# Split weights of seven tiles kept between two column parts of a decoder layer

## The chip, the cores and the metric

The kernel runs on one core of a Trainium2 chip. The metric is the device time of one execution in microseconds (us); a version is timed by the median of several runs.

Five engines with queues of their own work beside each other and meet at semaphores: TensorE (PE: matmuls, with its weight loads shown as PEld), VectorE (DVE), ScalarE (ACT), GpSimd (POOL) and SyncE (SP, which here issues nearly all loads from memory). Each queue is run in its written order: an instruction that waits holds up what stands behind it.

## The reference

One layer of a decoder: two branches (a gated linear recurrence and a chunked gated linear attention) are merged by learned gates into `m`; then come an output projection, a norm and a SwiGLU feed-forward net. The part that matters here is this:

```python
m = jax.nn.sigmoid(u_ga) * (y_a @ proj_a) + jax.nn.sigmoid(u_gb) * (y_b @ proj_b)
x = (x + gt1 * (m @ w_out)).astype(x.dtype)
h2 = _rmsnorm(x, norm2_g) * (1.0 + sc2) + sh2
f1, f2 = jnp.split(h2 @ ffn_w1, 2, axis=-1)
x = (x + gt2 * ((jax.nn.silu(f1) * f2) @ ffn_w2)).astype(x.dtype)
```

The model width is 1024, the hidden width of the feed-forward net is 2816. There are 1024 prompt tokens and 8 sequences of 4 sample tokens; everything is float32.

## The kernel before

Activations are kept transposed: features in the 128 partitions, tokens in the columns. The tokens go through the whole layer in two halves, A (512 prompt tokens) and B (512 prompt tokens and the 32 sample tokens). A tile name ends in the letter of its half: `woa` is the output projection's weight tile in half A, `wob` in half B.

A matrix product in float32 is made of three faster ones. An operand is split into a rounded high part and the rest: ACT copies it into the format `F32R` (the high part), and DVE subtracts that from the original (the low part). Three matmuls, high by high, high by low and low by high, make the product; in `gemm` they are lines 407, 408 and 409, and the third is the one that reads the low part of the weights. So a weight tile of 128x1024 costs one load of 512 KB into a buffer of the tag `raw` (5 buffers), one copy on ACT (line 150, with line 151 in `split_w`) and one subtraction on DVE (line 151) into a buffer of the tag `hl` (3 buffers). The `raw` buffer comes free when the subtraction is done, the `hl` buffer when the last matmul that uses it is done.

After the branches each half runs `merge_a` and then `back`. `merge_a` makes the eight tiles of `m`, one at a time, from a gate product (`gaps`, weights `gaps_hl`), and a product of 5 + 5 blocks (`paps`, weights `pa0`, `pa1`) with the ten tiles `ya`; the last, j = 7, ends with two operations on DVE (lines 1165 and 1166, on `ga7`) and the split of `m7` (ACT line 184, DVE line 185). `back` works on two column parts of the half, each 256 columns in A and 272 in B:

- `out_proj` on the first part (tiles `wo` of weights j = 0 to 7 in rising order), then on the second (j = 7 to 0). Each result gets the residual (`xr`, loaded for it by SP) added on DVE (line 1193 or 1182) and is squared on ACT for the norm.
- `norm2` of the first part, woven into the second part of `out_proj`, makes the eight tiles `h2` (DVE line 473, ACT line 486, DVE line 487).
- `ffn1_first` does the first four pairs of feed-forward tiles ("narrow couples", f = 0 to 3; weights `f1`, `f2`, results in `f1ps`, `f2ps`), first on part one, in rising order, with `norm2` of part two woven in; then on part two in falling order.

So each weight tile of `out_proj` and of the narrow couples is needed twice. `load_kept` lets the last three tiles before the turn stay in their `hl` buffers; all others are loaded and split a second time. That makes five tiles of `wo` (j = 4 to 0) and five of the couples (`f1` of f = 2, 1, 0 and `f2` of f = 1, 0) in each half.

Large tiles (two times 544 columns) come from a pool with the tag `S` and 17 buffers; `ya`, `yb`, `m`, the results `fa` of the couples and the blocks `t12`, `t4` of the next stage are all in it. A new tile takes the buffer that came free first, and its writer waits for the last reader of the tile that was there.

What is written is the program order; a scheduling layer then places the instructions in each engine's queue by their priority and by when it believes them ready. `tc.high_priority(AHEAD)` moves a piece 70 places forward in priority.

Of the kernel before, what the change touches and what calls it, by code (L numbers as in the profile page):

```python
# [7 lines left out]
F32 = mybir.dt.float32  # L8
F32R = mybir.dt.float32r
I32 = mybir.dt.int32  # L10
AF = mybir.ActivationFunctionType
# [6 lines left out]
KD = 8  # L18
# [11 lines left out]
EARLY = 4  # L30
FAST = 6
KORD = (0, 2, 4, 6, 1, 3, 5, 7)
AHEAD = 70
# [21 lines left out]
def hybrid_layer(ctx, tc, I, O):  # L55
    nc = tc.nc
    pe, act, dve, pool, sp = nc.tensor, nc.scalar, nc.vector, nc.gpsimd, nc.sync
# [21 lines left out]
    def S(name, dt=F32):  # L79
        return sbig.tile([P, 2 * 544], dt, tag="S", name=name)  # L80

    def T(name, w=544):
        return tp.tile([P, w], F32, tag="t", name=name)
# [12 lines left out]
    def mm(name):  # L96
        return mmk[1].tile([P, mmk[0], 512], F32, tag="mm", name=name)
# [41 lines left out]
    def load_raw(src, n, name):  # L139
        raw = wp.tile([P, 1024], F32, tag="raw", name=name + "_raw", bufs=5)  # L140
        sp.dma_start(raw[:, :n], src)
        return raw

    def load_w(src, n, name):
        return split_w(load_raw(src, n, name), n, name)

    def split_w(raw, n, name):
        hl = wp.tile([P, 2, 1024], F32R, tag="hl", name=name + "_hl", bufs=3)
        with tc.high_priority(AHEAD):
            act.activation(hl[:, 0, :n], raw[:, :n], AF.Copy)  # L150
            dve.tensor_sub(hl[:, 1, :n], raw[:, :n], hl[:, 0, :n].bitcast(F32))  # L151
        return hl

    held = {}

    def load_kept(key, src, n, name, last):

        if key in held:
            return held.pop(key)
        hl = load_w(src, n, name)  # L160
        if last:
            held[key] = hl
        return hl

    def split_apart(raw, n, name):

        hi, lo = S(name + "_hi", F32R), S(name + "_lo", F32R)
        act.activation(hi[:, :n], raw, AF.Copy)
        dve.tensor_sub(lo[:, :n], raw, hi[:, :n].bitcast(F32))
        return Apart(hi, lo)  # L170

    class Apart:
# [185 lines left out]
    class Half:  # L358
# [159 lines left out]
        def begin(s):  # L518
# [26 lines left out]
            def weights(i):  # L545
                hl[i] = (split_w if i < 3 else split_apart)(raws[i], 1024, f"early{ts[i]}")
# [650 lines left out]
        def out_proj(s, part, acc):  # L1197
            o, w = part[0], part[1]
            for q in range(KD):
                j = q if o == 0 else KD - 1 - q  # L1200
                n = f"{s.n}{o}{j}"
                xt = T("xr" + n)
                sp.dma_start(xt[:, :w], I["x" + s.n][:, j * s.N + o:j * s.N + o + w])
                ps = mm("wops" + n)
                s.gemm(ps, load_kept(("wo", j), I["w_out"][j], 1024, "wo" + n, o == 0 and j >= KD - 3), 8, s.m, part=part)
                if o == 0:
                    s.x.append(xp.tile([P, 544], F32, tag="X", name="xm" + n))
                with tc.high_priority(AHEAD):
                    s.residual(s.x[j], ps, 2, j, xt, part, "w" + n)
                    s.add_sq(acc, s.x[j][:, o:o + w], w, q, "2" + n)  # L1210
                yield w * 24 / 2400.0
# [9 lines left out]
        def pair(s, f, part, a):  # L1221

            n = f"{s.n}{f}{part[2]}{part[0]}"
            whole = part[2] is None
            gp = None if whole else part
            o, w = part[0], part[1]
            p1 = s.wide("f1ps" + n) if whole else mm("f1ps" + n)
            fr = not whole and o == 0
            s.gemm(p1, load_kept(("f1", f), I["ffn1"][2 * f], 1024, "f1" + n, fr and f == EARLY - 1), 8, s.h2, part=gp, order=KORD)
            yield w * 24 / 2400.0  # L1230
            tg = T("ft" + n)[:, :w]
            ps = [(tg[:, p[0] - o:p[0] - o + p[1]], p) for p in s.pieces(part)]
            for t, p in ps:
                act.activation(t, s.psv(p1, p), AF.Tanh, scale=0.5)
                dve.scalar_tensor_tensor(t, t, 1.0, s.psv(p1, p), op0=OP.add, op1=OP.mult)
            p2 = s.wide("f2ps" + n) if whole else mm("f2ps" + n)
            s.gemm(p2, load_kept(("f2", f), I["ffn1"][2 * f + 1], 1024, "f2" + n, fr and f >= EARLY - 2), 8, s.h2, part=gp, order=KORD)
            for t, p in ps:
                dve.tensor_mul(t, t, s.psv(p2, p))
            hi, lo = a[:, o:o + w], a[:, s.N + o:s.N + o + w]  # L1240
            act.activation(hi, tg, AF.Copy)
            dve.tensor_sub(lo, tg, hi.bitcast(F32))
            yield w * 24 / 2400.0

        def block_sums(s):
# [4 lines left out]
            for i in range(4):  # L1250
                h0, h1 = s.h2[2 * i], s.h2[2 * i + 1]
                d0, d1, ta, tb = [T(f"{c}{s.n}{i}") for c in ("d0", "d1", "ta", "tb")]
                for d, h in (d0, h0), (d1, h1):
                    dve.tensor_add(d[:, :N], h[:, :N].bitcast(F32), h[:, N:2 * N].bitcast(F32))
                dve.tensor_sub(ta[:, :W], d0[:, :W], d0[:, W:N])
                dve.tensor_sub(ta[:, W:N], d1[:, :W], ta[:, :W])
                dve.tensor_sub(tb[:, :W], d1[:, :W], d0[:, :W])
                dve.tensor_sub(tb[:, W:N], d1[:, W:N], ta[:, W:N])
                pair = lambda t: (t[:, :N], t[:, N:2 * N])
                if i == 0:  # L1260
                    t3 = pair(tp.tile([P, 2 * 544], F32R, tag="m2t", name="t3" + s.n, bufs=1))
                if i == 2:
                    t3 = [tp.tile([P, 544], F32R, tag="acc", name=f"t3{c}{s.n}", bufs=2) for c in "hl"]
                if i % 2 == 0:
                    t4 = pair(S(f"t4{s.n}{i}", F32R))
                t12 = pair(S(f"t12{s.n}{i}", F32R))
                o4 = i % 2 * W
                for t, o, src in (t12, 0, ta[:, :N]), (t4, o4, tb[:, W:N]), (t3, o4, tb[:, :W]):
                    w = N if t is t12 else W
                    act.activation(t[0][:, o:o + w], src, AF.Copy)  # L1270
                    dve.tensor_sub(t[1][:, o:o + w], src, t[0][:, o:o + w].bitcast(F32))
                for k, t, o in (("11", pair(h0), W), ("21", pair(h1), W), ("22", pair(h1), 0), ("t1", t12, 0), ("t2", t12, W),
                                ("t3", t3, o4), ("t4", t4, o4)):
                    s.bs[k].append((t[0][:, o:o + W], t[1][:, o:o + W]))
                yield 10
# [210 lines left out]
    p0, p1 = B.halves  # L1486
# [111 lines left out]
```

## Time and profile before

| | |
|---|---|
| median of 3 runs | 1983.96 us (1980.19 to 1984.69) |
| time of the profiled execution | 1982.02 us |
| its span, from first to last instruction | 1980.3 us |
| granted TensorE clock, mean | 0.994 |
| PE busy | 1948.1 us, 98% of the span |
| PEld busy | 1775.3 us, 90% |
| DVE busy | 1252.2 us, 63% |
| ACT busy | 914.9 us, 46% |
| read from memory | 259.16 MB |

PE is busy in all but 32 us of the span. A share over the whole span says little of one stage; the stage from `merge_a`'s end to the end of `ffn1_first` lies at about 551 to 664 us in half A and 1532 to 1650 us in half B. The matmul ends in the trace are modelled, so the distance between two starts is the better measure of PE's pace.

### The profile page before, as it was taken

Reading aid. Unit: us, or ns where it says so; the run is one execution under the profiler, and the core shown is the slowest. Engines: PE = TensorE matmul, PEld = TensorE weight load, DVE = VectorE, ACT = ScalarE, POOL = GpSimd, SP = SyncE. Lnnn points to the kernel's source line nnn. Section 1 sums busy time; section 2 is a strip of 40 time slices with the busy share of each in tenths; the row PEclk is TensorE's granted clock in tenths of the full one; section 3 lists DMA queues with packets and bytes.
Section 4 is the critical chain, followed back from the end, with each engine's and each line's share of the span. In section 5 each row is a group of like instructions: output and inputs, shape, how many; then the busy total and the mean of one; then the engine's idle time right before and its main releaser. Section 6 shows DMA issues by size and latency. Waiting matters only on the chain. (4 is left out here: it accounts for less than half of the span.)

```text
span 1980.3 us, 33359 instructions
## 1 busy us (share of the span) xinstructions
PE 1948.1 (98%) x13524; PEld 1775.3 (90%) x13524; DVE 1252.2 (63%) x2126; ACT 914.9 (46%) x1377; POOL 74.4 (4%) x159
## 2 busy tenths in 40 slices
PE   9999999999999999999999999999999999999998
PEld 5877877776899998998899999899999999999997
DVE  5648487656458764778563697774343687636776
ACT  3646475533235542555352465563232354415553
POOL 0000011000000000000000001010000000000000
PEclk9999999999999999999999999999999999999999
DMA  8334235566644457554413223323233434435553
GB/s 338 98 105 165 70 107 201 189 245 246 219 161 139 148 186 246 183 171 145 160 65 99 104 70 101 108 83 105 70 91 106 159 126 139 138 104 170 173 156 117
DMA packets 106906, 287.34 MB, mean 145 GB/s; under 512 B 12288, under 2 KB 20224, under 8 KB 106752
## 3 DMA queue, kind: packets, MB, share of 16 engines
q1 hardware_dynamic: 98608, 257.20, 39.9%
q0 software_dynamic: 7600, 27.45, 3.7%
q8 instruction: 106, 1.74, 0.4%
q10 hardware_dynamic: 544, 0.56, 0.1%
q14 instruction: 48, 0.39, 0.1%
HBM read 259.16 MB, written 26.01 MB: 144 GB/s over the span
## 5 line engine op out<-in xcount | busy, mean ns | idle before, releaser
L151 DVE TENSOR_TENSOR fwa_hl<-fwa,fwa_hl 128x1024 fp32r<-128x1024 f32 (+1 forms) x57 | 68.8, 1207 | 44.6 <-ACT fwa_hl L150 41.2
L151 DVE TENSOR_TENSOR fwb_hl<-fwb,fwb_hl 128x1024 fp32r<-128x1024 f32 (+1 forms) x57 | 68.7, 1206 | 39.9 <-ACT fwb_hl L150 35.5
L150 ACT ACTIVATE fwa_hl<-fwa 128x1024 fp32r<-128x1024 f32 (+1 forms) x57 | 59.2, 1039 | 44.0 <-PE fapsa L1305 10.8
L150 ACT ACTIVATE fwb_hl<-fwb 128x1024 fp32r<-128x1024 f32 (+1 forms) x57 | 59.3, 1040 | 33.3 <-PE fcpsb L1305 8.0
L150 ACT ACTIVATE f3b_hl<-f3b_raw 128x768 fp32r<-128x768 f32 (+1 forms) x45 | 35.7, 794 | 74.5 <-PE f3psb L409 21.4
L407 PE MATMUL f3psa<-faa,f3a_hl 128*128 128x512 f32 x176 | 68.7, 390 | 0.6 <-ACT f3a_hl L150 0.6
L409 PE MATMUL f3psa<-faa,f3a_hl 128*128 128x512 f32 x176 | 68.6, 390 | 0.4 <-DVE f3a_hl L151 0.4
L408 PE MATMUL f3psa<-faa,f3a_hl 128*128 128x512 f32 x176 | 68.6, 390 | 0.0
L151 DVE TENSOR_TENSOR f3b_hl<-f3b_raw,f3b_hl 128x768 fp32r<-128x768 f32 (+1 forms) x45 | 40.2, 892 | 35.9 <-ACT f3b_hl L150 34.7
L150 ACT ACTIVATE f3a_hl<-f3a_raw 128x768 fp32r<-128x768 f32 (+1 forms) x32 | 25.4, 792 | 55.7 <-PE f3psa L409 47.4
L409 PE MATMUL f3psb<-fab,f3b_hl 128*128 128x272 f32 x176 | 50.6, 288 | 0.0
L408 PE MATMUL f3psb<-fab,f3b_hl 128*128 128x272 f32 x176 | 50.5, 287 | 0.0
L407 PE MATMUL f3psb<-fab,f3b_hl 128*128 128x272 f32 x176 | 50.5, 288 | 0.0
L407 PE MATMUL uxpsb<-h1b,uxpsb_hl 128*128 128x256 f32 (+1 forms) x160 | 47.9, 299 | 0.1
L408 PE MATMUL uxpsb<-h1b,uxpsb_hl 128*128 128x256 f32 (+1 forms) x160 | 46.8, 293 | 0.0
L409 PE MATMUL uxpsb<-h1b,uxpsb_hl 128*128 128x256 f32 (+1 forms) x160 | 46.5, 290 | 0.0
L407 PE MATMUL ugpsb<-h1b,ugpsb_hl 128*128 128x272 f32 x160 | 46.3, 289 | 0.0
L409 PE MATMUL ugpsb<-h1b,ugpsb_hl 128*128 128x272 f32 x160 | 46.1, 288 | 0.0
L408 PE MATMUL ugpsb<-h1b,ugpsb_hl 128*128 128x272 f32 x160 | 45.8, 287 | 0.0
L407 PEld LDWEIGHTS f3psa<-faa,f3a_hl 128*128 128x128 f32 x176 | 33.1, 188 | 7.7 <-ACT f3a_hl L150 1.0
L409 PEld LDWEIGHTS f3psa<-faa,f3a_hl 128*128 128x128 f32 x176 | 33.1, 188 | 7.7 <-DVE f3a_hl L151 0.9
L408 PEld LDWEIGHTS f3psa<-faa,f3a_hl 128*128 128x128 f32 x176 | 33.1, 188 | 6.7
(1132 smaller groups left out, 7612.8 us busy)
## 6 DMA issues: line engine op xcount, KB each, us to landing
ada<-in_ada_w SPq DMA_DIRECT2D x48, 512.0 KB, 6.0
s_raw<-in_ffn SPq DMA_DIRECT2D x32, 512.0 KB, 3.9
wsum<-s_raw POOLq DMA_DIRECT2D x32, 512.0 KB, 3.6
fwa<-wsum SPq DMA_DIRECT2D x64, 256.0 KB, 3.3
fwb<-wsum SPq DMA_DIRECT2D x64, 256.0 KB, 3.3
fwa<-in_ffn SPq DMA_DIRECT2D x48, 256.0 KB, 3.1
fwb<-in_ffn SPq DMA_DIRECT2D x48, 256.0 KB, 3.0
f3b_raw<-in_ffn SPq DMA_DIRECT2D x23, 384.0 KB, 3.2
```

Source lines behind the costliest of these rows:

```text
L150: act.activation(hl[:, 0, :n], raw[:, :n], AF.Copy)
L151: dve.tensor_sub(hl[:, 1, :n], raw[:, :n], hl[:, 0, :n].bitcast(F32))
L407: pe.matmul(out, wh, x[:, o:o + w], start=st, stop=False)
L408: pe.matmul(out, wh, x[:, N + o:N + o + w], start=False, stop=False)
L409: pe.matmul(out, wl, x[:, o:o + w], start=False, stop=en)
```

## The change

`load_kept` gets an argument `apart`. A tile with `apart` is split not into an `hl` buffer but into two large tiles of the tag `S`, one for the high and one for the low part (`split_apart`), and stays there for the second column part. This holds for `wo` with j = 0 to 3, `f1` with f = 0 and 1, and `f2` with f = 0: seven tiles in each half. Their second load and split are gone. `split_apart`, which so far served one tile at the program's start, now has the raised priority that `split_w` had. The shift of lines by one from line 168 on comes from the added `with`.

```diff
-    def load_kept(key, src, n, name, last):
+    def load_kept(key, src, n, name, last, apart=False):
         if key in held:
             return held.pop(key)
-        hl = load_w(src, n, name)
-        if last:
+        hl = split_apart(load_raw(src, n, name), n, name) if apart else load_w(src, n, name)
+        if last or apart:
             held[key] = hl
         return hl
     def split_apart(raw, n, name):
         hi, lo = S(name + "_hi", F32R), S(name + "_lo", F32R)
-        act.activation(hi[:, :n], raw, AF.Copy)
-        dve.tensor_sub(lo[:, :n], raw, hi[:, :n].bitcast(F32))
+        with tc.high_priority(AHEAD):
+            act.activation(hi[:, :n], raw[:, :n], AF.Copy)
+            dve.tensor_sub(lo[:, :n], raw[:, :n], hi[:, :n].bitcast(F32))
         return Apart(hi, lo)
...
-                s.gemm(ps, load_kept(("wo", j), I["w_out"][j], 1024, "wo" + n, o == 0 and j >= KD - 3), 8, s.m, part=part)
+                s.gemm(ps, load_kept(("wo", j), I["w_out"][j], 1024, "wo" + n, o == 0 and j >= KD - 3, o == 0 and j < 4), 8, s.m, part=part)
...
-            s.gemm(p1, load_kept(("f1", f), I["ffn1"][2 * f], 1024, "f1" + n, fr and f == EARLY - 1), 8, s.h2, part=gp, order=KORD)
+            s.gemm(p1, load_kept(("f1", f), I["ffn1"][2 * f], 1024, "f1" + n, fr and f == EARLY - 1, fr and f < 2), 8, s.h2, part=gp, order=KORD)
...
-            s.gemm(p2, load_kept(("f2", f), I["ffn1"][2 * f + 1], 1024, "f2" + n, fr and f >= EARLY - 2), 8, s.h2, part=gp, order=KORD)
+            s.gemm(p2, load_kept(("f2", f), I["ffn1"][2 * f + 1], 1024, "f2" + n, fr and f >= EARLY - 2, fr and f < 1), 8, s.h2, part=gp, order=KORD)
```

The scheduling layer also orders the queues anew. Two places in half A follow; half B has the same ones with few differences. In the names, `woa00` is the tile j = 0 of `out_proj`'s first part in half A, `ga7` of half A is `gaa7`, and `ma7` is the last tile of `m`.

First place, where `merge_a` ends and `out_proj` begins. ACT's queue before:

```order
L150 ACTIVATE woa00_hl_4359<-woa00_raw_4357 128x1024
L1161 ACTIVATE gaa7_4304<-gapsa7_4274 128x512
L150 ACTIVATE woa01_hl_4394<-woa01_raw_4392 128x1024
L150 ACTIVATE woa02_hl_4431<-woa02_raw_4429 128x1024
L184 ACTIVATE ma7_4349<-gaa7_4304 128x512
```

ACT's queue with the change:

```order
L1162 ACTIVATE gaa7_4304<-gapsa7_4274 128x512
L150 ACTIVATE woa04_hl_4509<-woa04_raw_4507 128x1024
L150 ACTIVATE woa05_hl_4546<-woa05_raw_4544 128x1024
L185 ACTIVATE ma7_4349<-gaa7_4304 128x512
L169 ACTIVATE woa00_hi_4359<-woa00_raw_4357 128x1024
L169 ACTIVATE woa01_hi_4395<-woa01_raw_4393 128x1024
L169 ACTIVATE woa02_hi_4433<-woa02_raw_4431 128x1024
```

DVE's queue at the same place before:

```order
L151 TENSOR_TENSOR woa00_hl_4359<-woa00_raw_4357,woa00_hl_4359 128x1024
L151 TENSOR_TENSOR woa01_hl_4394<-woa01_raw_4392,woa01_hl_4394 128x1024
L1165 SCALAR_TENSOR_TENSOR gaa7_4304<-gaa7_4304,papsa7_4306 128x512
L1166 TENSOR_TENSOR gaa7_4304<-gaa7_4304,mba7_3611 128x512
L151 TENSOR_TENSOR woa02_hl_4431<-woa02_raw_4429,woa02_hl_4431 128x1024
L185 TENSOR_TENSOR ma7_4349<-gaa7_4304,ma7_4349 128x512
```

DVE's queue with the change:

```order
L151 TENSOR_TENSOR woa04_hl_4509<-woa04_raw_4507,woa04_hl_4509 128x1024
L1166 SCALAR_TENSOR_TENSOR gaa7_4304<-gaa7_4304,papsa7_4306 128x512
L151 TENSOR_TENSOR woa05_hl_4546<-woa05_raw_4544,woa05_hl_4546 128x1024
L1167 TENSOR_TENSOR gaa7_4304<-gaa7_4304,mba7_3611 128x512
L186 TENSOR_TENSOR ma7_4349<-gaa7_4304,ma7_4349 128x512
L170 TENSOR_TENSOR woa00_lo_4360<-woa00_raw_4357,woa00_hi_4359 128x1024
L170 TENSOR_TENSOR woa01_lo_4396<-woa01_raw_4393,woa01_hi_4395 128x1024
```

The splits of the tiles 0 and 1, which PE uses first, stood ahead of the work on `ga7` and `m7` and now stand behind it; the splits of the tiles 4 and 5 went ahead. In half B, DVE has the subtraction of tile 5 ahead of both operations on `ga7`; the rest is alike. PE's queue there now begins so:

```order
L410 MATMUL papsa7_4306<-yaa9_3481,pa1a7_hl_4329 128x512
L408 MATMUL wopsa00_4356<-ma0_3753,woa00_hi_4359 128x256
L409 MATMUL wopsa00_4356<-ma0_3753,woa00_hi_4359 128x256
L408 MATMUL wopsa01_4392<-ma0_3753,woa01_hi_4395 128x256
L410 MATMUL wopsa00_4356<-ma0_3753,woa00_lo_4360 128x256
```

Before, 22 matmuls of tile 0 stood there in a row; now the fourth matmul needs the low part of tile 0, and the third the high part of tile 1.

Second place, in `ffn1_first`, between the pairs f = 0 (`f1psa000`, `f2psa000`, whose product becomes `faa0`) and f = 1. ACT's queue with the change:

```order
L1235 ACTIVATE fta000_4997<-f1psa000_4966 128x256
L1242 ACTIVATE faa0_4965<-fta000_4997 128x256
L169 ACTIVATE f1a100_hi_5055<-f1a100_raw_5053 128x1024
L1235 ACTIVATE fta100_5083<-f1psa100_5052 128x256
L150 ACTIVATE f1a300_hl_5215<-f1a300_raw_5213 128x1024
```

DVE's queue with the change, from the second norm's first operation on (`rs_2a256` and `ri_2a256` hold the reciprocal root of `norm2`'s second part):

```order
L303 TENSOR_SCALAR rs_2a256_5038<-nps2a256_5034 128x2
L1240 TENSOR_TENSOR fta000_4997<-fta000_4997,f2psa000_5000 128x256
L304 TENSOR_SCALAR ri_2a256_5039<-rs_2a256_5038 128x2
L307 SCALAR_TENSOR_TENSOR rs_2a256_5038<-rs_2a256_5038,ri_2a256_5039 128x2
L308 TENSOR_TENSOR rs_2a256_5038<-rs_2a256_5038,ri_2a256_5039 128x2
L310 SCALAR_TENSOR_TENSOR rs_2a256_5038<-rs_2a256_5038,ri_2a256_5039 128x2
L1243 TENSOR_TENSOR faa0_4965<-fta000_4997,faa0_4965 128x256
L307 SCALAR_TENSOR_TENSOR rs_2a256_5038<-rs_2a256_5038 128x2
L308 TENSOR_TENSOR rs_2a256_5038<-rs_2a256_5038 128x2
L310 SCALAR_TENSOR_TENSOR rs_2a256_5038<-rs_2a256_5038 128x2
L307 SCALAR_TENSOR_TENSOR rs_2a256_5038<-rs_2a256_5038 128x2
L170 TENSOR_TENSOR f1a100_lo_5056<-f1a100_raw_5053,f1a100_hi_5055 128x1024
```

Before, the split of `f1a100` stood on DVE between the residual of the last but one `wo` tile and the last three tiles of `h2`:

```order
L1193 SCALAR_TENSOR_TENSOR xma01_4421<-wopsa2561_4896,gains_122,xra2561_4894 128x256
L151 TENSOR_TENSOR f1a100_hl_5069<-f1a100_raw_5067,f1a100_hl_5069 128x1024
L442 TENSOR_TENSOR acc21a_4353<-acc21a_4353,sq2a2561_4927 128x256
L473 SCALAR_TENSOR_TENSOR xn2a05_4930<-xma05_4569,gains_122,rb2a0_4795 128x256
```

It left the chain of the first norm and went behind the whole of pair 0 and into the chain of the second norm. On PE, pair 1 in turn moved: before, 9 of its matmuls stood among those of pair 0; now all 48 of pair 0 come first, then the norm's small matmuls (`nps2a256`), then 2 with `f1a100_hi`, 9 of `f2psa100`, and then the first with `f1a100_lo`.

## The prediction, made before the change was run

> **What bounds the kernel now.** I read the page first, then the stretches of the stage that is changed, then single instructions in it. The page:
>
> ```profile
> span 1980.3 us, 33359 instructions
> PE 1948.1 (98%) x13524; PEld 1775.3 (90%) x13524; DVE 1252.2 (63%) x2126; ACT 914.9 (46%) x1377; POOL 74.4 (4%) x159
> ```
>
> PE is the bound: all its idle time is 1980.3 - 1948.1 = 32 us, and work taken from ACT, DVE or SP can only shorten the kernel where PE waits for it. The view by stretches shows where (columns: the stretch, its length, PE busy and its matmuls, PEld, DVE, ACT, POOL, granted PE clock, DMA share, GB/s):
>
> ```profile
> 558.00:582.00 24.00, 24.00 (x202) 23.90 (x201) 14.22 (x21) 9.44 (x14) 0.00 (x0) 1.00 0.57 193
> 605.00:608.00 3.00, 2.88 (x25) 2.67 (x23) 1.72 (x6) 1.06 (x1) 0.00 (x0) 1.00 0.82 266
> 608.00:612.00 4.00, 2.25 (x13) 1.85 (x14) 3.81 (x8) 1.73 (x4) 0.00 (x0) 0.97 0.48 170
> 612.00:616.00 4.00, 4.00 (x24) 4.00 (x23) 0.74 (x2) 1.34 (x3) 0.00 (x0) 0.61 0.06 19
> 1552.00:1562.00 10.00, 10.00 (x83) 10.00 (x82) 5.44 (x9) 3.19 (x5) 0.00 (x0) 1.00 0.68 218
> 1590.00:1594.00 4.00, 3.57 (x28) 3.23 (x27) 3.74 (x8) 2.60 (x5) 0.00 (x0) 1.00 0.55 165
> 1594.00:1598.00 4.00, 2.19 (x16) 1.77 (x15) 3.40 (x11) 1.29 (x3) 0.00 (x0) 1.00 0.53 167
> ```
>
> While `out_proj` runs, PE does 202 matmuls in 24 us (8.4 per us, half A) and 83 in 10 us (8.3, half B) without a gap, though ten tiles are split beside it. The only losses lie where the narrow couples begin. Half A, 605 to 616 us: 62 matmuls, worth 62/8.4 = 7.4 us, take 11 us, so 3.6 us are lost. Half B, 1590 to 1598 us: 44 matmuls, worth 5.3 us, take 8, so 2.7 us are lost. Part of A's loss is the clock: it fell to 0.61 after the gaps, and 24 matmuls took 4 us where 2.85 would do, a price of 1.15 us for one such drop.
>
> The rows of these gaps, first DVE and PE of A, then PE of B:
>
> ```profile
> 607.48 0.48 DVE L1193 SCALAR_TENSOR_TENSOR xma<-wopsa,gains,xra 128x256 f32<-128x256 f32 x1 [1.28 <-DMA xra<-in_xa]
> 607.88 1.22 DVE L151 TENSOR_TENSOR f1a_hl<-f1a_raw,f1a_hl 128x1024 fp32r<-128x1024 f32 x1
> 609.15 0.39 PE L409 MATMUL f1psa<-h2a,f1a_hl 128*128 128x256 f32 x1 [1.27 <-DVE f1a_hl L151]
> 610.82 0.39 PE L407 MATMUL f1psa<-h2a,f1a_hl 128*128 128x256 f32 x1 [0.57 <-ACT h2a L486]
> 1596.34 0.39 PE L407 MATMUL f1psb<-h2b,f1b_hl 128*128 128x272 f32 x1 [1.81 <-ACT h2b L486]
> ```
>
> DVE's queue is late there: it waits for a residual, then does a split of 1.22 us, and the last tiles of `h2` come after that.
>
> **What is removed.** Two groups of splits, and their loads in the window where `out_proj` starts (KB each, median us to landing):
>
> ```profile
> L150 ACT ACTIVATE woa_hl<-woa_raw x13: 1043/1060/1061, 551.3 to 596.9; 128x1024 fp32r<-128x1024 f32 x13
> L151 DVE TENSOR_TENSOR woa_hl<-woa_raw,woa_hl x13: 1215/1224/1226, 552.4 to 599.5; 128x1024 fp32r<-128x1024 f32 x13
> woa_raw<-in_w_out SPq DMA_DIRECT2D x12, 512.0 KB, 3.5
> ```
>
> Of 13 splits of `wo` in each half 9 are left. Over both halves 14 go: 14 x 1.06 = 14.8 us of ACT, 14 x 1.22 = 17.1 us of DVE, 14 loads of 512 KB. Where PE runs without a gap this is worth nothing, since PE itself is the cover. It is worth something at the start of the couples: the second parts' splits of `wo` and that of `f1a100` no longer stand among the first norm's operations. Following the new DVE queue, the last `h2` tiles of A need, after the residual of tile j = 1, three steps of the norm and their remainders, about 3.5 us after PE begins the couples; PE has 18 matmuls before it needs `h2` 6 and nine more before it needs the last (27 x 0.12 = 3.2 us). So I take nearly the whole loss as regained: 3.6 us in A, 2.7 in B. Bounds: nothing, if the residuals' loads hold DVE up as they do now, and all 6.3.
>
> **What is added: the start of `out_proj`.** The new queues set the two splits PE needs first behind `m7`, whose inputs are `merge_a`'s last matmuls. Half A now (PE, ACT, DVE, then SP's issue of the loads that take the next free buffers):
>
> ```profile
> 557.62 0.39 PE L409 MATMUL papsa<-yaa,pa1a_hl 128*128 128x512 f32 x1
> 557.84 0.28 PE L407 MATMUL wopsa<-ma,woa_hl 128*128 128x256 f32 x1
> 558.19 0.28 PE L407 MATMUL wopsa<-ma,woa_hl 128*128 128x256 f32 x1
> 551.29 1.06 ACT L150 ACTIVATE woa_hl<-woa_raw 128x1024 fp32r<-128x1024 f32 x1 [2.52 <-PE gapsa L409]
> 552.25 0.58 ACT L1161 ACTIVATE gaa<-gapsa 128x512 f32<-128x512 f32 x1
> 559.49 0.63 ACT L184 ACTIVATE ma<-gaa 128x512 fp32r<-128x512 f32 x1 [0.34 <-DVE gaa L1166]
> 558.04 0.69 DVE L1165 SCALAR_TENSOR_TENSOR gaa<-gaa,papsa 128x512 f32<-128x512 f32 x1 [1.03 <-PE papsa L409]
> 558.76 0.69 DVE L1166 TENSOR_TENSOR gaa<-gaa,mba 128x512 f32<-128x512 f32 x1
> 553.63 10.88 SPq L141 DMA_DIRECT2D woa_raw<-in_w_out  x4
> ```
>
> Today PE goes over to `out_proj` without a gap, since two tiles are ready, and the fourth matmul starts at 558.19. With the change, by these durations: ACT does `gaa7` from 551.3 and the high part of tile 4 to 552.9; DVE subtracts to 554.1; only then does tile 5 get its buffer, and its load lands at 554.1 + 3.5 = 557.6, so its high part is there at 558.7. DVE does the first operation on `gaa7` at 558.04 as now, then tile 5's subtraction (1.22) to 559.9, then the second operation to 560.6. ACT can then make `m7`'s high part (561.2), tile 0's (562.3) and tile 1's (563.3). DVE subtracts for tile 0 from 562.3 to 563.5. PE's fourth matmul, the first to read a low part, starts at 563.5 and not at 558.19: 5.3 us. Queued behind on ACT are tiles 2 and 3, which PE needs 6 and 9 us later, so one gap it is.
>
> Half B:
>
> ```profile
> 1532.57 1.05 ACT L150 ACTIVATE wob_hl<-wob_raw 128x1024 fp32r<-128x1024 f32 x1
> 1533.65 1.23 DVE L151 TENSOR_TENSOR wob_hl<-wob_raw,wob_hl 128x1024 fp32r<-128x1024 f32 x1 [3.50 <-ACT wob_hl L150]
> 1534.90 11.47 SPq L141 DMA_DIRECT2D wob_raw<-in_w_out  x4
> 1539.52 0.72 DVE L1165 SCALAR_TENSOR_TENSOR gab<-gab,papsb 128x544 f32<-128x544 f32 x1 [1.37 <-PE papsb L409]
> 1540.38 0.36 PE L407 MATMUL wopsb<-mb,wob_hl 128*128 128x272 f32 x1 [0.91 <-DVE gab L1165]
> ```
>
> Tile 4 takes the place of tile 0, so tile 5 is loaded from 1534.9 and lands at 1538.4; ACT is done with it at 1539.5, DVE, which has it ahead of `gab7` here, at 1540.7. The two operations on `gab7` end at 1542.1, ACT's `m7` at 1542.8 and tile 0 at 1543.8, DVE's tile 0 at 1545.0. The fourth matmul stood at 1540.38 + 0.45 = 1540.8: 4.2 us.
>
> PE idles some 5 us in a row in both halves, so I add a drop of the clock to each at 1.15 us. The trace has it both ways: after 1.75 us idle in 608 to 612 the clock fell; after 1.81 us in 1594 to 1598 it did not, nor after 2.45 us here:
>
> ```profile
> 1176.00:1180.00 4.00, 1.55 (x15) 1.32 (x13) 4.00 (x7) 2.04 (x4) 0.00 (x0) 1.00 0.48 153
> ```
>
> A gap of 5 us is twice the longest of these, so I count the drop; without it each half is 1.15 us better. [...]
>
> **What is added: between pairs 0 and 1.** The split of `f1a100` now waits until `faa0` is made. The rows for it, the norm's small matmuls in A and B and DVE's small steps:
>
> ```profile
> 617.49 0.54 PE L414 MATMUL nps2a<-ones,acc21a 128*128 128x1 f32 x4
> 1601.75 0.83 PE L414 MATMUL nps2b<-ones,acc21b 128*128 128x1 f32 x6
> 618.14 0.41 DVE L1239 TENSOR_TENSOR fta<-fta,f2psa 128x256 f32<-128x256 f32 x1
> 624.34 0.15 DVE L309 SCALAR_TENSOR_TENSOR rs_2a<-rs_2a 128x2 f32<-128x2 f32 x1
> 624.52 0.16 DVE L306 SCALAR_TENSOR_TENSOR rs_2a<-rs_2a 128x2 f32<-128x2 f32 x1
> ```
>
> From the end of pair 0's matmuls in A: 0.54 for the norm's matmuls, then on DVE nine small steps of 0.2 (start to start), two of 0.4 (the product and `faa0`'s remainder), and 1.22 for the subtraction: 0.54 + 1.8 + 0.8 + 1.2 = 4.3 us. ACT's side (`faa0`, then the high part) is ready at 2.5. PE has 0.54 + 11 x 0.12 = 1.9 us of work, so it waits 2.4 us. In B DVE starts the product beside the norm's matmuls: 0.83 + 8 x 0.2 + 0.4 + 1.2 = 4.0, less 0.83 + 10 x 0.125 = 2.1: 1.9 us. Bounds: 0, if the split gets done during pair 0 after all, and 3.6 each with a drop of the clock.
>
> **What only moves.** On SP the residual `xra02` stands behind the loads for three couples, which wait for buffers until the split of tile 3, at about 568 us. It should land some 4 us later, while PE needs until 563.5 + 72 x 0.12 + 1.15 = 573.3 for tiles 0 to 2. Costed at nothing; if it is late, PE still has three free accumulators, some 9 us.
>
> **The sum.** A: 5.3 + 1.15 + 2.4 - 3.6 = 5.3 us. B: 4.2 + 1.15 + 1.9 - 2.7 = 4.6 us. Together 9.9 us more than the profiled execution: span 1990.2, time 1982.0 + 9.9 = 1991.9. That execution was 1.9 us under the median of the three; against the median it is 1993.9. I forecast 1993 us, slower by 0.5%.
>
> **The rivals.** (1) Faster: the splits of tiles 0 to 3 hide in `merge_a`'s last product, where ACT has a gap of 2.5 us, and only the 6.3 us remain, as a gain: 1975.7, or 1977.7 against the median. For it speaks that buffers of `ya` come free tile by tile during that product; against it that the queues are in order and stand otherwise. It decides if the fourth matmul is less than about 1 us late. 0.07. (2) No change that can be told (within 0.2%, 4 us, which is about what a measurement of this kernel can tell): the starts cost 9.5, but the clock stays up and pair 1's split is done in time, so 9.5 - 6.3 = 3.2 us: 1985.2 or 1987.2. 0.13. (3) Worse: the residuals' loads, which now stand behind the loads for the second part, hold DVE up before the last `h2` tiles, and the 3.6 and 2.7 stay lost: 9.9 + 6.3 = 16 us, 1998 or 2000. For it speaks DVE's wait of 1.28 us for such a load today; it decides if the residual of tile 1 lands over 1 us after tile 0's matmuls begin. 0.15. (4) That the change removes nothing is out: its queues lack the 14 splits and loads. The forecast has 0.65, with a range of its own of 1989 to 1997.
>
> **Chances.** Faster 0.07, same 0.13, slower 0.65 + 0.15 = 0.80. Left out of 1986.5 to 2000 are rival 1, the lower part of 2 and the far end of 3.
>
> **What would show it.** In the changed profile: PE idle for 4 to 5.5 us ahead of the first matmul with `woa_lo` and `wob_lo`, put down to ACT `wo_hi` or DVE `wo_lo`; the clock under 1 in the 4 us after it; waits of PE for `f1_hi` or `f1_lo` of some 2 us; none left for `h2`. I am wrong if PE goes over from `paps` to `wops` with less than 2 us of idle time.

## The result, and the profile after

| | median | runs | ratio to the kernel before, 95% interval |
|---|---|---|---|
| before, beside it | 1984.03 us | 6 | |
| changed | 1995.67 us (1991.92 to 2001.2) | 6 | 1.0066 (1.0051 to 1.0081) |
| changed, a second time | 1993.88 us (1988.75 to 1997.45) | 5 | 1.0050 (1.0034 to 1.0065) |

The change makes the kernel slower, by 11.6 us the first time and by 10.5 us the second (1993.88 - 1983.35, the median before beside those runs). The forecast was 1993 us, slower by 0.5%, with 1986.5 to 2000 as its range. The profiled execution took 1992.05 us. The head of its page:

```profile
span 1990.3 us, 33290 instructions
PE 1947.4 (98%) x13524; PEld 1775.6 (89%) x13524; DVE 1238.3 (62%) x2112; ACT 901.4 (45%) x1363; POOL 74.7 (4%) x159
```

DVE and ACT do 14 operations fewer each (2126 to 2112, 1377 to 1363), and are busy 13.9 and 13.5 us less. PE's work is the same, and the span is 10.0 us longer. In the two pages all of it looks like idle time of PE, 32 us before and 43 now, but that is chance: by the view by stretches, in the stages that the change touches (the table of stages below) PE idles 8.4 us more and is busy 4.3 us longer with the same matmuls, and in the rest of the span it was busy 5.0 us less in this execution. The view of PE's waits (total, times, longest) puts names to it:

```profile
PE wopsa L408 <- ACT woa_hi L169: 4.6, 2, 4.1
PE wopsb L408 <- ACT wob_hi L169: 4.1, 1, 4.1
PE f1psa L408 <- ACT f1a_hi L169: 2.0, 1, 2.0
PE f1psb L408 <- ACT h2b L487: 1.6, 1, 1.6
PE f1psb L408 <- ACT f1b_hi L169: 1.4, 1, 1.4
```

None of the four waits for a `_hi` tile is there before the change. The start of `out_proj` in half A, DVE and ACT and then PE, in order of time:

```profile
557.16 1.06 ACT L150 ACTIVATE woa_hl<-woa_raw 128x1024 fp32r<-128x1024 f32 x1 [4.78 <-DMA woa_raw<-in_w_out]
558.25 1.23 DVE L151 TENSOR_TENSOR woa_hl<-woa_raw,woa_hl 128x1024 fp32r<-128x1024 f32 x1
559.39 0.68 DVE L1167 TENSOR_TENSOR gaa<-gaa,mba 128x512 f32<-128x512 f32 x1
560.11 0.63 ACT L185 ACTIVATE ma<-gaa 128x512 fp32r<-128x512 f32 x1 [1.89 <-DVE gaa L1167]
560.64 2.94 ACT L169 ACTIVATE woa_hi<-woa_raw 128x1024 fp32r<-128x1024 f32 x3
561.71 3.50 DVE L170 TENSOR_TENSOR woa_lo<-woa_raw,woa_hi 128x1024 fp32r<-128x1024 f32 x3 [0.25 <-ACT woa_hi L169]
561.73 0.39 PE L408 MATMUL wopsa<-ma,woa_hi 128*128 128x256 f32 x1 [4.14 <-ACT woa_hi L169]
562.68 0.42 PE L408 MATMUL wopsa<-ma,woa_hi 128*128 128x256 f32 x1 [0.44 <-ACT woa_hi L169]
562.99 0.58 PE L410 MATMUL wopsa<-ma,woa_lo 128*128 128x256 f32 x1
```

ACT sits idle for 4.78 us until tile 5's load has landed, although the weights of tiles 0 and 1 are not yet split: those splits stand behind `m7` in its queue, and `m7` stands behind DVE's subtraction for tile 5. The first matmul with a low part starts at 562.99.

The clock comes next. The view by stretches, cut at edges 3.413 us apart (why there is told at the end), columns as in the prediction:

```profile
559.48:562.89 3.41, 0.71 (x3) 0.48 (x3) 2.46 (x4) 2.78 (x4) 0.00 (x0) 1.00 0.46 154
562.89:566.30 3.41, 3.41 (x16) 3.31 (x16) 3.41 (x5) 2.58 (x3) 0.00 (x0) 0.50 0.72 183
566.30:569.72 3.42, 3.42 (x31) 3.42 (x30) 1.58 (x3) 0.42 (x1) 0.00 (x0) 1.00 0.94 315
617.50:620.92 3.42, 1.45 (x13) 1.36 (x13) 2.31 (x13) 1.36 (x2) 0.00 (x0) 1.00 0.02 5
620.92:624.33 3.41, 3.41 (x18) 3.41 (x18) 1.29 (x3) 0.00 (x0) 0.00 (x0) 0.50 0.32 108
1542.52:1545.93 3.41, 0.73 (x6) 0.51 (x5) 2.58 (x3) 0.73 (x2) 0.00 (x0) 1.00 0.15 25
1545.93:1549.34 3.41, 1.81 (x6) 1.47 (x7) 2.69 (x3) 3.41 (x5) 0.00 (x0) 0.50 0.33 131
1549.34:1552.76 3.42, 3.42 (x17) 3.42 (x17) 3.42 (x4) 1.79 (x2) 0.00 (x0) 0.50 0.87 230
1607.37:1610.78 3.41, 2.04 (x18) 1.95 (x17) 2.23 (x11) 1.38 (x2) 0.00 (x0) 1.00 0.00 0
1610.78:1614.20 3.42, 3.42 (x18) 3.42 (x17) 1.34 (x5) 0.00 (x0) 0.00 (x0) 0.50 0.45 152
```

After each of the four gaps (two at `out_proj`, two at couple 1) the clock is at half for one such stretch, after the gap at `out_proj` of half B for two. The second profile of the changed kernel has two slow stretches after each gap at `out_proj`, one after the gap at couple 1 of A, and none after the one in B, which is 1.38 us long in both profiles (by its view at 4 us edges: 0.65 and 0.50 in 560 to 568, 0.81, 0.50 and 0.84 in 1552 to 1564, 0.83 and 0.75 in 620 to 628, 1.00 in 1612 to 1624). A busy stretch at half clock costs half its length, 1.7 us: PE does 16 to 18 matmuls in it, and 31 (A, 566.30 to 569.72) or 29 (B, 1552.76 to 1556.17) in a stretch at full clock.

**The stages.** From the first and last starts of PE's tiles in the tile view the span is cut into seven parts: the beginning to the last `papsa` matmul (557.6 us before), `out_proj` of A (to the first `f1psa`, 47.7), couples and norm of A (to the first `fapsa`, 73.4), the middle (to the last `papsb`, 860.5), `out_proj` of B (to the first `f1psb`, 50.9), couples of B (to the first `fapsb`, 78.3), and the rest (311.9). The differences from the kernel before's first profile, in us:

| kernel | beginning | out_proj A | couples A | middle | out_proj B | couples B | rest |
|---|---|---|---|---|---|---|---|
| changed | -0.4 | +6.2 | +0.3 | -2.3 | +6.0 | +0.3 | -0.1 |
| changed, again | +1.1 | +6.3 | +0.1 | +3.7 | +6.3 | -2.0 | -0.1 |
| before, again | +3.8 | 0.0 | -2.0 | -0.3 | -0.2 | +1.3 | -0.1 |
| e1: wo only | -0.5 | +6.5 | -4.1 | +1.2 | +6.6 | -3.2 | +0.8 |
| e2: couples only | +3.6 | 0.0 | +6.7 | -1.9 | -0.3 | +6.0 | -0.1 |
| e3b: wo 2 to 4 | +4.1 | 0.0 | -1.6 | -1.5 | -0.5 | +3.2 | +0.2 |
| e4: wo 2 to 4, couple 0 | +1.2 | -0.1 | -4.0 | -1.8 | -0.5 | -3.0 | +0.1 |
| e5: couple 0 only | +2.2 | 0.0 | -0.4 | -0.5 | +0.3 | +2.7 | +0.2 |
| e6: wo apart, not kept | +3.3 | +6.8 | -1.7 | -0.1 | +6.1 | -0.2 | 0.0 |
| e7: wo 2 to 4 only | +4.0 | -0.4 | -3.5 | +0.5 | -0.5 | +0.3 | +0.4 |
| e8: wo 1 to 4, couple 0 | -0.7 | +3.5 | -4.7 | -0.6 | +2.1 | -1.2 | +0.2 |
| e9: change, couple 0 only | +4.8 | +6.1 | -4.5 | -1.1 | +5.9 | -4.7 | +0.2 |
| e12: change, written earlier | +1.0 | +0.5 | -4.0 | -0.2 | +2.3 | -4.3 | -0.2 |

The order of the queues is the same in all these kernels until some 7 us before the end of the beginning, and no edit lies in the middle; yet these two move by up to 4.8 us from one profile to the next. So a total from one profile says little, and the four stages of the change say much (rounded starts make each entry good to 0.1 us): `out_proj` repeats within 0.3 us, the couples within 2.3 us. In the changed kernel these four come to +12.8 us, and to +10.7 the second time.

### The profile page after: what moved, and what is told of

Same layout as the page of the kernel before. It is cut to its first block, busy times and chain, and to the rows that moved or that the text cites. A ratio compares the mean times of both kernels' runs of the same rounds, so it can differ in the third digit from the quotient of the medians.

```text
span 1990.3 us, 33290 instructions
## 1 busy us (share of the span) xinstructions
PE 1947.4 (98%) x13524; PEld 1775.6 (89%) x13524; DVE 1238.3 (62%) x2112; ACT 901.4 (45%) x1363; POOL 74.7 (4%) x159
```

## The experiments

Theory 1: the loss is made where a split stands in the queues. The splits of tiles 0 and 1 stand behind `m7`, that of couple 1's `f1` behind `faa0`, and PE waits for them; the tiles kept are harmless, and their saving is real. Theory 2: the tiles kept are what costs, because they hold large buffers through both column parts. Theory 3, for the first two runs: the couples alone cause the loss. All edits are shown against the changed kernel.

**e1 and e2: the two parts of the change, each alone.** e1 turns off the couples, e2 the output projection.

```diff
 # e1, in pair, for f1 and for f2
-fr and f == EARLY - 1, fr and f < 2)
+fr and f == EARLY - 1, False)
-fr and f >= EARLY - 2, fr and f < 1)
+fr and f >= EARLY - 2, False)
 # e2, in out_proj
-o == 0 and j >= KD - 3, o == 0 and j < 4)
+o == 0 and j >= KD - 3, False)
```

> Only the four wo tiles are split apart and kept; the couples' weights are as before. Theory 1 (the loss is made at the two starts of out_proj, where the splits of tiles 0 and 1 stand behind m7): both gaps of 4.1 us stay, with the slow clock behind them, +12 us between merge_a's end and out_proj's end over both halves; at the couples the waits for h2 shrink and f1a100's split stands before pair 0 again, -4 to -5 us; total +7, about 1991 us. Theory 2 (tiles that stay in large buffers hold up what needs them next, and the loss is spread over second parts and couples): the loss scales with the tiles kept, 8 of 14, so about +6.5 with the couples no better. By the totals the two are close; they part in the rows: theory 1 wants +12 before the couples and a gain in them, theory 2 wants couples as slow as in the changed kernel. Theory 3 (the couples' weights alone cause the loss): 1984 us or less.

Measured: 1991.18 us, ratio 1.0052 (1.0037 to 1.0068). `out_proj` costs 13.1 us, the couples gain 7.3. PE's waits there:

```profile
PE wopsa L408 <- ACT woa_hi L169: 4.3, 2, 4.1
PE wopsb L408 <- ACT wob_hi L169: 4.1, 1, 4.1
```

The same two gaps as in the changed kernel, and no wait for `h2` or `f1` but one of 0.5 us: theory 1 in its rows, and a gain larger than it had.

> Only f1 of couples 0 and 1 and f2 of couple 0 are split apart and kept; wo is as before. Theory 1: no gap at the starts of out_proj (under 1 us in each half); pair 1 waits about 2 us for f1_hi in half A and 1.4 in B, with a slow clock of about 1.5 us behind each; the waits for h2 shrink by about 1 us in each half since the split of f1a100 leaves the norm's chain: total +3 to +5, about 1988 us. Theory 2: the loss scales with the tiles kept, 6 of 14, about +5, with waits spread and no single one over 1 us. Theory 3 (the couples' weights alone cause the loss): +10, about 1994 us.

Measured: 1997.99 us, ratio 1.0084 (1.0053 to 1.0114), slower than the whole change. `out_proj` is as before; the couples lose 12.7 us, where theory 1 had 3 to 5. The total, 15.9 us above the kernel before, is beyond all three theories; it comes nearest to theory 3 (+10), which fails at e1, where `out_proj` alone loses as well. PE's waits:

```profile
PE f1psa L408 <- ACT h2a L487: 4.3, 2, 2.3
PE f1psb L408 <- ACT h2b L487: 3.5, 3, 2.4
PE f1psa L408 <- ACT f1a_hi L169: 2.0, 1, 2.0
PE f1psb L408 <- ACT f1b_hi L169: 1.4, 1, 1.4
PE f1psb L409 <- DVE h2b L488: 1.3, 1, 1.3
```

The waits for `f1_hi` are as forecast; the waits for `h2` grew, where I had them shrink. e9 and e5 were made to tell why.

**e3b and e4: other tiles.** Both keep wo tiles 2, 3 and 4 in place of 0 to 3, so that tiles 0 and 1 have their splits as before the change; e4 also leaves `f1` of couple 1 as before.

```diff
 # e3b and e4, in out_proj
-o == 0 and j < 4)
+o == 0 and 2 <= j < 5)
 # e4 alone, in pair, for f1
-fr and f < 2)
+fr and f < 1)
```

> As the changed kernel, but wo tiles 2, 3 and 4 are kept apart in place of 0 to 3 (tiles 0 and 1 are split as before the change, and loaded again for the second part). Theory 1: PE has the 48 matmuls of tiles 0 and 1 (5.8 us) while tiles 2 and 3 are split, so the gaps at the starts go from 4.1 us to under 1, the clock stays up there, and of the change's +11.6 us only what happens in the couples is left: +0 to +2, about 1985 us. Theory 2: six tiles kept in place of eight in this place, loss of 8 to 10 us, about 1993 us.

Measured: 1988.46 us, ratio 1.0029 (1.0013 to 1.0045). Both gaps at `out_proj` are gone (0.0 and -0.5 us), with six of the eight large tiles of `wo` still kept: theory 2 is out for this stage. What is left in the stages of the change is in the couples, +1.6 us, with the waits for `f1_hi` (1.6 and 1.4 us) that e2 has too. The total does not fit that: the median is 6.4 us above the kernel before, where theory 1 had 0 to 2. The beginning was 4.1 us longer in the profile; what the other runs paid is not shown.

> As the kernel with tiles 2, 3 and 4 of wo kept apart, and f1 of couple 1 is split as before the change as well, so that only couple 0's two tiles are kept apart there. Theory 1: no gap at the starts, no wait of pair 1 for f1_hi and no slow clock behind it; what is left is the gain at the start of the couples, 3 us in A and 1 to 2.7 in B: -4 to -6 us, about 1979 us, faster than before. Theory 2: 10 of 14 tiles kept, loss of 6 to 8 us, about 1991 us.

Measured: 1975.21 us, ratio 0.9969 (0.9957 to 0.9981), faster than before. One tile less, and the couples go from +1.6 to -7.0 us. The start of `out_proj` and that of the couples in half A, from the view by stretches:

```profile
558.00:562.00 4.00, 4.00 (x32) 3.81 (x31) 2.93 (x5) 2.42 (x3) 0.00 (x0) 1.00 0.39 131
608.00:616.00 8.00, 7.91 (x65) 7.78 (x65) 6.75 (x20) 2.87 (x7) 0.00 (x0) 1.00 0.38 135
```

In these 12 us PE idles for 0.09 and the clock stays up.

**e6: apart, but not kept.** Place without keeping, the couples as before the change.

```diff
-        if last or apart:
+        if last:
             held[key] = hl
```

(and the two lines of e1.)

> The four wo tiles are split apart into large tiles, but given up after the first column part, so the second part loads and splits all of them again as before the change; the couples' weights are as before. Theory 1 (the large tiles come from buffers that merge_a's last product still reads, and their splits stand behind m7; keeping them is harmless): the starts of out_proj cost +12 us over both halves as in the changed kernel, the couples gain nothing: +11 to +13, about 1994 us. Theory 2 (tiles held through both parts are what costs): 0, about 1982 us.

Measured: 1995.12 us, ratio 1.0078 (1.0062 to 1.0094). `out_proj` loses 6.8 and 6.1 us though none of the four tiles outlives its first column part. Theory 2 falls here: the four tiles cost as much without being kept.

**e7: wo tiles 2 to 4 and nothing else.** (e3b's line and e1's two.)

> Wo tiles 2, 3 and 4 are kept apart, and the couples' weights are all as before the change. If the gain of 7 us at the couples that the run with tiles 2 to 4 and couple 0 showed comes from wo alone (theory 1: splits of wo gone from the first norm): -6 to -8 us, about 1975 us. If couple 0's two kept tiles bring a part of it: -2 to -5, about 1979 us.

Measured: 1981.14 us, ratio 0.9997 (0.9984 to 1.0010): no change that can be told. The couples gain 3.5 us in A and lose 0.3 in B, where PE still waits for `h2` and `f1`. So couple 0's two tiles bring a part of e4's gain, and theory 1 as I had put it, that wo alone brings it, was wrong.

**e9: the change with one tile less.** (e4's second line alone.)

> The changed kernel with one tile less: f1 of couple 1 is split as before the change. Theory 1 (that one tile, behind faa0 in the queues, costs its wait of 2.0 and 1.4 us and the slow clock behind each): the couples go from +0.6 to -7 us against before, the starts of out_proj stay at +12: +5, about 1987 us, 7 to 8 less than the changed kernel. If the couples lose for another reason (all kept tiles, the DMA queue): within 2 us of the changed kernel, 1993 us or more.

Measured: 1989.15 us, ratio 1.0046 (1.0031 to 1.0061), 4 runs. By the stages it came as forecast, and more: couples -9.2 us, `out_proj` +12.0. The total is 4 us above what these stages give; its beginning was 4.8 us longer, and whether that is this program's or chance its runs don't settle. Against the changed kernel's two profiles the one tile, `f1` of couple 1, costs 4.6 to 4.8 us in A and 2.7 to 5.0 in B, far above its waits of 2.0 and 1.4.

**e5: couple 0 alone.** (e2's line and e4's second.)

> Only couple 0's two tiles are kept apart, wo and couple 1 as before the change. If the loss of 12.7 us at the couples in the run with the couples alone was mainly the late split of couple 1's f1 (2.0 and 1.4 us of waits and their slow stretches): no wait for f1_hi, couples within 2 us of before, total 1983 us. If it was the small split buffers that couple 0 gives up, which let the splits of couple 1 and 2 come forward into the first norm's chain beside wo's: the waits for h2 stay at 3 to 5 us in each half, couples +3 to +4 in each half, total about 1989 us.

Measured: 1985.05 us, ratio 1.0004 (0.9994 to 1.0015), the couples -0.4 and +2.7 us. Beside e2 (+6.7 and +6.0) this says that 10.4 of the 12.7 us that e2 loses come from couple 1's `f1`: nearer the first of the two cases, though the 2.3 us left are a little over its 2. In B, 2.7 us of PE's waits are put down to a residual operation of `out_proj` on DVE (`fxwb`, line 1186); why it is late there is open. In half A, DVE does as many splits at the same places of the norm in both (some of other tiles) and finishes `h2` about 10 us behind the couples' start in both; what differs is PE's queue. Of the first couples' matmuls in half A, the seventh and the tenth in e5 and then the seventh to the ninth in e2 (`f1a_hl` is couple 1's here, `f1a_hi` couple 0's):

```profile
608.23 0.28 PE L408 MATMUL f1psa<-h2a,f1a_hl 128*128 128x256 f32 x1
609.11 0.36 PE L408 MATMUL f2psa<-h2a,f2a_hl 128*128 128x256 f32 x1 [0.36 <-DVE xma L1194]
```

```profile
612.03 0.39 PE L408 MATMUL f1psa<-h2a,f1a_hi 128*128 128x256 f32 x1 [2.25 <-ACT h2a L487]
612.26 0.28 PE L408 MATMUL f2psa<-h2a,f2a_hi 128*128 128x256 f32 x1
613.29 0.39 PE L409 MATMUL f1psa<-h2a,f1a_hi 128*128 128x256 f32 x1 [0.75 <-DVE h2a L488]
```

Where couple 1's `f1` is split in time, its matmuls with the first `h2` tiles fill a part of the time until the next `h2` tiles are made. Where its split stands behind `faa0`, couple 1 can't be woven into couple 0, and PE waits longer for `h2`: 5.1 us in A in e2, 1.6 in e5. The view by stretches shows it, e5 (22 matmuls, though the clock fell) and then e2 (12 at full clock):

```profile
612.00:616.00 4.00, 3.93 (x22) 3.93 (x23) 2.87 (x9) 1.24 (x3) 0.00 (x0) 0.63 0.66 202
```

```profile
612.00:616.00 4.00, 2.03 (x12) 1.61 (x12) 3.05 (x7) 1.22 (x4) 0.00 (x0) 1.00 0.82 259
```

**e8: how much cover is enough.** Tiles 1 to 4 kept apart, couple 0 as in e4, so that tile 0 alone covers the start.

```diff
-o == 0 and j < 4)
+o == 0 and 1 <= j < 5)
```

> As the run with wo tiles 2 to 4 and couple 0 (1975 us), but tile 1 is kept apart as well, so that PE has the 24 matmuls of tile 0 alone (2.9 us) while tile 1 is split behind m7. A gap of about 4.6 - 2.9 = 1.7 us is left at each start. If the clock falls only after gaps of 4 us as in the changed kernel: 2 x 1.5 = +3 on that run, about 1978 us. If a gap of under 2 us is enough for the clock to fall: 2 x 3 = +6, about 1981 us.

Measured: 1981.41 us, ratio 1.0008 (0.9995 to 1.0021). `out_proj` +3.5 and +2.1 us, 6.2 more than e4. PE's rows with a wait in A (of the timeline), then the stretches:

```profile
560.66 0.38 PE L408 MATMUL wopsa<-ma,woa_hl 128*128 128x256 f32 x1 [0.91 <-ACT ma L185]
561.39 0.39 PE L409 MATMUL wopsa<-ma,woa_hl 128*128 128x256 f32 x1 [0.34 <-DVE ma L186]
562.56 0.38 PE L408 MATMUL wopsa<-ma,woa_hi 128*128 128x256 f32 x1 [0.43 <-ACT woa_hi L169]
```

```profile
560.04:563.45 3.41, 2.01 (x12) 1.60 (x12) 2.55 (x4) 3.41 (x5) 0.00 (x0) 1.00 0.34 136
563.45:566.87 3.42, 3.42 (x19) 3.42 (x18) 3.17 (x3) 2.79 (x5) 0.00 (x0) 0.50 0.73 193
```

Three short waits, 1.7 us together, 1.4 of it within the first of these stretches, were enough for the clock to fall, and the slow stretch costs another 1.7. In B it is one wait of 1.99 us (0.91 before the change) for DVE's first operation on `gab7`, and the clock falls behind it too (0.61 in 1540 to 1544). So the second case holds: the price of this small gap about doubles.

**e12: the whole change, written in another order.** All seven tiles are kept as in the change, but the splits of wo tiles 0 and 1 are written ahead of `m7`, and that of couple 1's `f1` ahead of couple 0's product. In the program a large buffer goes to the writer that comes first. Ten tiles `ya` and seven of `m` are as many as the 17 large buffers, so by this count `m7` takes the first buffer of `ya` that `merge_a`'s last product gives back, and the two tiles' splits come after it; no view shows the buffers themselves.

```diff
 # in load_kept, with ready = {}
+        if key in ready:
+            held[key] = ready.pop(key)
+            return held[key]
 # new
+    def early(key, src, name):
+        ready[key] = split_apart(load_raw(src, 1024, name), 1024, name)
 # in merge_a, behind the last product, before m is made
+                if j == KD - 1:
+                    for t in range(2):
+                        early(("wo", t), I["w_out"][t], f"wo{s.n}0{t}")
 # in pair, behind f1's product
+            if fr and f == 0:
+                early(("f1", 1), I["ffn1"][2], f"f1{s.n}100")
```

> The whole change with all its kept tiles, only written in another order: the splits of wo tiles 0 and 1 are written ahead of m7 (behind merge_a's last product), that of f1 of couple 1 ahead of couple 0's product, so that they take their large tiles earlier. In the queues wo 0 and 1 then stand ahead of m7, and f1a100's split among the first norm's operations. Theory 1 (place in the queues, not the kept tiles): the gap of 4.1 us ahead of wops goes; m7 now stands behind the splits of tiles 5 and 6, whose loads land late, so PE waits about 2 us for m7 within tile 0, with or without a slow stretch of 1.7 us: out_proj +2 to +4 in each half in place of +6; no wait for f1_hi: couples -4 to -5 in each half as in the run without that tile; together 0 to -5, about 1979 us. Theory 2 (the kept tiles themselves): as the changed kernel, +12, about 1994 us.

Measured: 1979.81 us, ratio 0.9982 (0.9971 to 0.9994). The same tiles kept, the same 14 splits and loads gone, and the loss of 10 to 12 us is a small gain: keeping the tiles is not the cause, the order in which their splits are written is. That order sets both the buffer that a split takes and its place in the queue, and this run does not part the two; in the changed kernel's rows above, ACT does tile 0 right behind `m7`, so at that moment the queue held it, not a buffer. In A the splits of tiles 0 and 1 now stand in the gap that ACT had during `merge_a`'s last product:

```profile
553.63 2.00 ACT L175 ACTIVATE woa_hi<-woa_raw 128x1024 fp32r<-128x1024 f32 x2
```

There `out_proj` loses only 0.5 us, where theory 1 had 2 to 4; in B it loses 2.3, by two waits. The second is for `m7`, which now stands behind tile 6's load. The first is for DVE's first operation on `gab7`, which stands behind the subtraction for tile 5; PE waited 0.91 us for the same operation before the change:

```profile
1538.70 0.36 PE L414 MATMUL wopsb<-mb,wob_hi 128*128 128x272 f32 x1 [1.91 <-DVE gab L1172]
1542.58 0.52 PE L414 MATMUL wopsb<-mb,wob_hi 128*128 128x272 f32 x2 [1.00 <-ACT mb L191]
```

**The two kernels again.** No edit.

> The changed kernel once more, for its time on the chip of these runs and a second profile. If the differences before merge_a's end and between the halves (-0.4 and -2.3 us in its first profile) are chance: another value between -1 and +5 and between -2.5 and +1.5 here, with out_proj at +12 and the couples within 1.5 us of +0.6 again. If they belong to the program: the same two values.

> The kernel before once more, for a second profile. If the stages that no edit touches vary by chance: the time to merge_a's end differs by some us from 557.6, the stages of the change by under 1 us each from their first values.

Measured: the changed kernel 1993.88 us; the kernel before 1982.90 us, ratio to the other runs of it 0.9993 (0.9982 to 1.0003). Beginning and middle came out with other values (+1.1 and +3.7; +3.8 and -0.3), so they vary from execution to execution, the middle by more than I had said (up to +1.5). The stages of the change repeat, but the couples less well than I had said: in the kernel before -2.0 us in A and +1.3 in B. Rows of its view by stretches, in A and in B:

```profile
612.00:616.00 4.00, 3.28 (x23) 2.88 (x24) 2.77 (x8) 1.31 (x3) 0.00 (x0) 1.00 0.53 169
1600.00:1604.00 4.00, 4.00 (x26) 4.00 (x25) 1.44 (x2) 1.99 (x4) 0.00 (x0) 0.71 0.00 0
```

The first profile had its slow clock in A (0.61 in 612 to 616) and none in B; this one has none in A and 0.71 in B. The same program pays for it in one execution here and in another there.

## Why the prediction was right, and where it was not

**Sign, size and place held.** Forecast: span +9.9 us; measured +10.0 in the profile, +11.6 and +10.5 in the medians. That the span came out within 0.1 us is luck: the stages that no step speaks of gave back 2.8 us (-0.4, -2.3, -0.1), and those of the steps lost 12.8.

**The start of `out_proj` (forecast 11.8 us, measured 12.2).** The working of the queues held row by row: `m7`, tile 0 and tile 1 follow one another on ACT behind tile 5, as said, and the first matmul with a low part started at 562.99; forecast was 563.5, and `merge_a`'s last matmul stood 0.4 us earlier in this profile. The gap was put down to ACT `wo_hi`, as named. Two terms were mis-sized against each other. The delays were forecast at 5.3 and 4.2 us; PE's idle time grew by 4.6 in A and by 3.4 in B, where the old wait of 0.91 falls away. The drop of the clock was forecast at 1.15 us each, from one row cut at 4 us edges; it is 1.7 in A, and in B two slow stretches in which PE is busy for 1.81 + 3.42 us, half of it 2.6; in the second profile both halves have two slow stretches.

**Between couples 0 and 1 (forecast 2.4 and 1.9 us): mis-sized.** The waits measured 1.97 and 1.38 us, but in the first profile each was followed by a slow stretch of 1.7 us (in the second only the one in A), which I had only in the bounds, and the step missed a second effect: a split that comes late takes couple 1's matmuls away as filler for the waits for `h2` (e5 beside e2). Without that tile the couples are 7.3 to 9.8 us better (e9), where the step had 4.3.

**What is removed (forecast 6.3 us regained): too small.** Where nothing is late the couples gain 7.3 (e1), 7.0 (e4) and 9.2 us (e9). In the changed kernel the two steps together came to +0.6 and, again, -1.9 us, where the forecast had 4.3 - 6.3 = -2.0. Two errors, up to 5.5 us on the loss and 2.9 on the gain, stood against each other here.

**What only moves** was costed at nothing, and `out_proj` shows no wait for it. In the norm of B, DVE waited 1.12 us for a residual:

```profile
1602.06 0.47 DVE L1183 SCALAR_TENSOR_TENSOR xmb<-wopsb,gains,xrb 128x240 f32<-128x240 f32 x1 [1.12 <-DMA xrb<-in_xb]
```

That is rival 3's mechanism, and PE's wait of 1.55 us for `h2b` comes behind it; in the second profile that wait was 0.5. It did not decide, but the sign "none left for `h2`" did not hold in B.

**The rivals.** The splits did not hide in the last product (rival 1: the gap would have to be under 1 us, it is 4.1); e12 shows that they do when they are written ahead of `m7`. Rival 2 needed the clock to stay up and couple 1 in time; neither happened.

## What to carry to other kernels

A split, copy or load that is kept longer must still be issued as early as the one it replaces: what decided here was not the 14 splits saved (27 us of DVE and ACT, which waited anyway) but three in each half that moved behind another result in the queues of ACT and DVE (PE waited 4.1 us for them at each start of `out_proj`, 2.0 and 1.4 us ahead of couple 1). Look first at which buffer the new tile takes and who gives it back, then at what stands ahead of its writer; a longer-lived tile belongs where the bounding engine has other work while it is made (tiles 0 to 3 of `wo` alone: 0.5% slower; tiles 2 to 4 alone: no change that can be told, and with couple 0's two tiles 0.3% faster). And weigh a gap by what it does to the clock behind it and to work that could have been woven in, not by its own length alone (e8 in A: 1.7 us of waits, and 1.7 more in the slow stretch behind them).

## What the runs showed of the hardware

Cut at edges 3.4133 us apart, counted from one fall of the clock, all 582 stretches of the changed kernel's profile have a granted clock of exactly 1.00 (574) or 0.50 (8), and so have all 579 of the kernel before's first profile (573 and 6). The spacing is read from the trace: the slow stretches of the changed kernel are 3.41 us long or twice that, but for one that runs to the end of the span, and from the fall at 562.89 to the rise at 1614.20 it goes 308 times. So in these two profiles each change of the clock lies on one of these edges, wherever the gap ahead of it begins; a stretch between two edges is a beat in what follows. I had expected a long gap to be needed for a fall; in these runs the length of a gap doesn't tell. 1.97 us ahead of couple 1 was enough, and so was 1.7 us in three pieces, of which 1.4 lay within one beat (e8). 1.38 us ahead of couple 1 in B was enough in the changed kernel's first profile, where it lay in one beat, and not in its second, where it lay over two (an estimate: counted on from the clock's rise at 1561.3 an edge falls at 1615.9, and PE idles for 0.42 us in 1612 to 1616 and 0.96 in 1616 to 1620). And 2.45 us of idle time in one piece in the kernel before, which fell over two beats (3.41 - 2.54 and 3.42 - 1.84), did not bring the clock down:

```profile
1174.94:1178.35 3.41, 2.54 (x19) 2.09 (x17) 3.41 (x6) 3.10 (x5) 0.56 (x1) 1.00 0.14 47
1178.35:1181.77 3.42, 1.84 (x11) 1.71 (x12) 3.42 (x8) 0.00 (x0) 0.00 (x0) 1.00 0.49 152
1181.77:1185.18 3.41, 3.41 (x26) 3.25 (x26) 1.49 (x4) 3.32 (x5) 0.32 (x2) 1.00 0.35 129
```

Nor is the share of busy time the measure. In the changed kernel a beat with 2.54 us of PE busy was followed by one at half clock; 20 of its 22 matmuls have a single column:

```profile
1262.62:1266.04 3.42, 2.54 (x22) 2.39 (x21) 2.80 (x4) 3.22 (x5) 0.00 (x0) 1.00 0.96 333
1266.04:1269.45 3.41, 3.41 (x10) 2.60 (x9) 2.75 (x10) 0.79 (x2) 0.00 (x0) 0.50 0.03 12
```

In the changed kernel's profile and the kernel before's first one, from about 7 us on, where their clock records begin, 32 beats at full clock have PE busy for under 80%, and 10 of them have a slow beat behind them. All eight whose matmuls, counted by their starts, had 1,796 columns together or fewer (by the shapes in the profile) are among the 10; of the other 24, with 2,128 to 6,032 columns, two are, those with 2,454 and 3,072. Columns alone don't decide either: at 9.93 us of the changed kernel's profile a beat with 1,545 columns, in which PE was busy for 2.86 us, was not followed by a slow one. What else decides is open.

The second surprise is how much of a time is not the kernel's: the beginning, in which these programs differ at most in the last 7 us, took 556.9 to 562.4 us over the 14 profiles. PE idled 8.1 us of it in the kernel before's first profile, with two slow beats, and 11.0 in the changed kernel's, with none.
